# Choosing experts among 64 sums, four heads at a time, with Pool left out

## The chip, the cores and the metric

One Trainium2 chip, one core of it. The time is that of one execution of the whole program in microseconds on the device; three runs were taken, and the median stands for the kernel. Engines are named as in the profile: PE is TensorE, DVE is VectorE, ACT is ScalarE, POOL is GpSimd, SP issues most DMAs.

## What is computed

Two model blocks run one after the other on 512 tokens of width 1024. The change concerns the last part alone, a layer of experts (PEER). Each token has 8 heads. For each head two query halves are scored against 128 keys each; the best 16 of either side are taken, all 256 sums of one from each side are formed, and the best 16 sums name 16 experts and, by a softmax, their gates.

```python
s1, i1 = lax.top_k(sc[:, :, 0], 16)
s2, i2 = lax.top_k(sc[:, :, 1], 16)
cand = (s1[..., :, None] + s2[..., None, :]).reshape(ntok, 8, 256)
best, pos = lax.top_k(cand, 16)
e1 = take_along_axis(i1, pos // 16); e2 = take_along_axis(i2, pos % 16)
idx = e1 * 128 + e2                      # one of 16384 experts
gate = softmax(best)
act = gelu(u_tab[idx] . t) * gate        # per token: 128 experts
out = sum(act * v_tab[idx])
```

## The kernel before

The kernel is written in Tile: each instruction is put on an engine by hand, and the framework orders each engine's instructions by program order and by when their inputs are expected to be ready. An engine takes its queue in order, so an instruction that waits holds up what is behind it; instructions of a later part of the program may be placed ahead of earlier ones that are not ready yet.

The 512 tokens of the expert layer are four blocks of 128. Three of them (n = 0, 1, 2) take the dense way: for each of the 128 groups j of 128 experts, a first product of `u` with the 384 tokens and a GELU (`first_product`, L1724, 24 matmuls), the product with a gate matrix, and a second product with `v` that is summed up in PSUM (L1887). The fourth block (n = 3) gathers its experts' rows by indirect DMA and works on VectorE (L1846 to L1871).

Weights come in 128x1024 f32 tiles through `load_w` (L227 to L245): a DMA, a high half by ScalarE (L243), and a low half by a subtract (L244), which stands on VectorE unless `sub` names another engine. Of the three products that TensorE makes with each weight, one reads that low half.

The expert part has these stages.

1. Queries and scores (L1637 to L1767). `head_queries` makes the queries of a head from two weights, subtracted on Pool. For each head h and block n two matmuls give 128 tokens x 2 x 128 scores (L1750). For n = 0 in all heads, and for n = 1, 2 in heads 0 to 3, `choose` follows at once; the other scores are copied aside, those of n = 3 too. Nine first products (`FILLS`) are put between, subtracted on Pool.

2. `choose` (L1674) for one head: two searches for the best 16 of 128 (each two MAX8, two FIND_INDEX8 and a MATCH_REPLACE8), the 256 sums (L1691), a third search over these (L1693), the split of a position into its two flags (L1695 to L1699), a one-hot compare of both over 512 bf16 elements (L1701), a multiply with the keys on Pool (L1703) and a sum over the flags (L1704).

3. `spread` (L1770), for n = 0, 1, 2 in turn: softmax of the best sums (`soften`), three transposes, and then 32 steps. A step takes four tokens: VectorE makes two one-hot tiles of 128x512 (L1783, L1784), the gate is multiplied into the first (in even steps by four ScalarE scalings, L1787; in odd ones by Pool, L1789), four matmuls give the tokens' 128x128 gate matrices (L1804), and ScalarE copies them to a stage tile (L1806) that goes to memory every eighth step. The one-hots run two steps ahead of the matmuls; each of the two has five buffers. Between the steps stand 21 first products and, in the steps with k % 8 == 4, the `choose` of a waiting head of block n + 1.

4. Second products with gathers (L1837 to L1927). `prepare` loads the gates of four expert groups at a time, multiplies them into the activations (L1882, the gates at a step of four elements), splits the result and loads the `v` weight. Between them stand the remaining first products and the gathers of the fourth block, whose eight heads are chosen one by one from the scores kept aside.

Of the kernel before, what the change touches and what calls it, by code (L numbers as in the profile page):

```python
# [185 lines left out]
def _program(tc, I, out, dbg, upto, layers, pools):  # L186
# [1434 lines left out]
    ND = 3  # L1621
# [8 lines left out]
    gd = dr.tile([ND, 128, 32, 128, 4], F32, name="gd")  # L1630
# [30 lines left out]
    def sixteens(pool):  # L1661

        t = pool.tile([128, 16, 16], BF16, name="iob")
        nc.gpsimd.iota(t, pattern=[[1, 16], [0, 16]], base=0, channel_multiplier=0,
                       allow_small_or_imprecise_dtypes=True)
        return t

    def selection(pool, bufs):

        best = pool.tile([128, 8, 16], F32, name="best", tag="best", bufs=bufs)  # L1670
        keys = pool.tile([128, 2, 8, 16], F32, name="keys", tag="keys", bufs=bufs)
        return best, keys

    def choose(pool, sel, h, sc):  # L1674

        best, keys = sel
        s2 = pool.tile([128, 256], F32, name="s2", tag="s2", bufs=1)
        vv = pool.tile([128, 2, 16], F32, name="vv", tag="vv", bufs=2)
        ii = pool.tile([128, 3, 16], U32, name="ii", tag="ii", bufs=2)

        def top16(v, i, src, tmp):
            nc.vector.max(v[:, 0:8], src)
            nc.vector.max_index(i[:, 0:8], v[:, 0:8], src)
            nc.vector.match_replace(tmp, v[:, 0:8], src, -3.0e38)
            nc.vector.max(v[:, 8:16], tmp)
            nc.vector.max_index(i[:, 8:16], v[:, 8:16], tmp)

        for s in range(2):
            top16(vv[:, s], ii[:, s], sc[:, s], s2[:, 128 * s:128 * s + 128])
        cd = pool.tile([128, 256], F32, name="cd", tag="cd", bufs=1)  # L1690
        nc.vector.tensor_tensor(cd.rearrange("p (a b) -> p a b", a=16), vv[:, 0, :, None].to_broadcast([128, 16, 16]),  # L1691
                                vv[:, 1, None, :].to_broadcast([128, 16, 16]), op=OP.add)
        top16(best[:, h], ii[:, 2], cd, s2)  # L1693
        ab = pool.tile([128, 2, 16], U32, name="ab", tag="ab", bufs=2)
        nc.vector.tensor_scalar(ab[:, 0], ii[:, 2], 4, None, op0=OP.logical_shift_right)  # L1695
        nc.vector.tensor_scalar(ab[:, 1], ii[:, 2], 15, None, op0=OP.bitwise_and)
        fl = pool.tile([128, 2, 2, 16], BF16, name="fl", tag="fl", bufs=2)
        nc.vector.tensor_copy(fl[:, 0], ab)
        nc.vector.tensor_copy(fl[:, 1], ii[:, 0:2])  # L1699
        oh = pool.tile([128, 2, 16, 16], BF16, name="oh", tag="oh", bufs=2)  # L1700
        nc.vector.tensor_tensor(oh, iob[:, None].to_broadcast([128, 2, 16, 16]),  # L1701
                                fl[:, 0, :, None, :].to_broadcast([128, 2, 16, 16]), op=OP.is_equal)
        nc.gpsimd.tensor_tensor(oh, oh, fl[:, 1, :, :, None].to_broadcast([128, 2, 16, 16]), op=OP.mult)  # L1703
        nc.vector.tensor_reduce(keys[:, :, h], oh.rearrange("p s j k -> p s k j"), axis=AX.X, op=OP.add)  # L1704
# [28 lines left out]
    iob = sixteens(p1)  # L1733
# [35 lines left out]

    def spread(n):  # L1770
        best, keys = sels[n]
# [21 lines left out]
        for k in range(32 + LEAD):  # L1793
# [5 lines left out]
            if m % 8 == 0:  # L1799
                st = p1.tile([128, 32, 32, 4], F32, name="stg", tag="stage", bufs=2)  # L1800
# [5 lines left out]
            nc.scalar.activation(st[:, :, t0:t0 + 4], pg4.rearrange("p (t g e) -> p g t e", t=4, e=4), AF.Copy)  # L1806
            yield
            if m % 8 == 7:
                q = m // 8
                nc.sync.dma_start(gd[n, :, :, 32 * q:32 * q + 32], st)  # L1810
# [9 lines left out]
    steps, w = 0, None  # L1820
    for n in range(ND):
        for k, _ in enumerate(spread(n)):
            if steps in plan:
                first_product(plan[steps], w=w)
            steps += 1
            if steps + AH in plan and n == 2:
                w = load_w(I["uT"][plan[steps + AH]])
            elif steps + AH in plan:
                w = load_w(I["uT"][plan[steps + AH]], sub=SUB)
# [8 lines left out]
    iob = sixteens(p2)  # L1838
# [7 lines left out]
    def gather_head(h):  # L1846
        choose(p2, gsel, h, SC[:, 2 * h:2 * h + 2])
# [120 lines left out]
```

## Time and profile before

| | |
|---|---|
| median of 3 runs | 3669.14 us (3663.05 to 3673.33) |
| profiled execution | 3662.47 us, its span 3660.7 us |
| PE busy | 3516.7 us (96%) |
| DVE busy | 2413.3 us (66%) |
| ACT busy | 1494.5 us (41%) |
| POOL busy | 954.5 us (26%) |
| mean granted clock | 0.983 of 2.4 GHz |

Busy times are unions of an engine's instructions; on PE they say that something was in the array, not that it ran at its best. The rows of the waits say how long the first engine stood still for the second, in how many places. The stages lie in the span like this: queries and scores from 2280 us to about 2447, spread to 2699, three last first products to 2714, second products and gathers to the end.

### The profile page before, as it was taken

Reading aid. Unit: us, or ns where it says so; the run is one execution under the profiler, and the core shown is the slowest. Engines: PE = TensorE matmul, PEld = TensorE weight load, DVE = VectorE, ACT = ScalarE, POOL = GpSimd, SP = SyncE. Lnnn points to the kernel's source line nnn. Section 1 sums busy time; section 2 is a strip of 40 time slices with the busy share of each in tenths; the row PEclk is TensorE's granted clock in tenths of the full one; section 3 lists DMA queues with packets and bytes.
Section 4 is the critical chain, followed back from the end, with each engine's and each line's share of the span. In section 5 each row is a group of like instructions: output and inputs, shape, how many; then the busy total and the mean of one; then the engine's idle time right before and its main releaser. Section 6 shows DMA issues by size and latency. Waiting matters only on the chain. (4 is left out here: it accounts for less than half of the span.)

```text
span 3660.7 us, 54336 instructions
## 1 busy us (share of the span) xinstructions
PE 3516.7 (96%) x21341; PEld 3187.1 (87%) x21341; DVE 2413.3 (66%) x4258; ACT 1494.5 (41%) x2675; POOL 954.5 (26%) x722
## 2 busy tenths in 40 slices
PE   8999999999999999999989999987889999999998
PEld 8999999999898877888868877877788999999987
DVE  6565344334857545443477745788989988888865
ACT  4464233223346433332342633335653444443433
POOL 4221120000512202000133221455433433333321
PEclk9999999999999999999999999998999999999999
DMA  4102232222320233223331031324479888888855
GB/s 135 65 30 75 94 122 87 93 88 92 117 81 30 68 105 127 92 93 97 104 105 53 30 109 64 113 84 133 139 219 348 328 320 312 312 316 325 321 203 181
DMA packets 185888, 531.43 MB, mean 145 GB/s; under 512 B 16416, under 2 KB 70048, under 8 KB 168992
## 3 DMA queue, kind: packets, MB, share of 16 engines
q1 hardware_dynamic: 150272, 367.67, 30.6%
q0 software_dynamic: 18432, 134.23, 9.2%
q10 hardware_dynamic: 16928, 26.06, 2.2%
q8 instruction: 168, 2.75, 0.3%
q14 instruction: 88, 0.72, 0.1%
HBM read 492.64 MB, written 35.19 MB: 144 GB/s over the span
## 5 line engine op out<-in xcount | busy, mean ns | idle before, releaser
L243 ACT ACTIVATE whi<-wraw 128x1024 fp32r<-128x1024 f32 x594 | 627.8, 1058 | 1048.6 <-PE g L263 636.6
L244 DVE TENSOR_TENSOR wlo<-wraw,whi 128x1024 fp32r<-128x1024 f32 x543 | 680.1, 1253 | 296.3 <-ACT whi L243 282.3
L263 PE MATMUL g<-uh,whi 128*128 128x264 f32 (+1 forms) x1864 | 470.9, 315 | 4.4 <-ACT z L617 3.2
L263 PE MATMUL g<-uh,wlo 128*128 128x264 f32 (+1 forms) x1864 | 465.0, 312 | 1.3 <-DVE wlo L244 1.3
L263 PE MATMUL g<-ul,whi 128*128 128x264 f32 (+1 forms) x1864 | 465.3, 312 | 0.0
L350 POOL TENSOR_TENSOR ssq<-ssq,sq 128x512 f32<-128x512 f32 (+2 forms) x84 | 131.9, 1570 | 924.3 <-issue 716.7
L1730 PE MATMUL f<-TH,wlo 128*128 128x384 f32 x1024 | 349.9, 342 | 5.6 <-POOL wlo L244 5.6
L1730 PE MATMUL f<-TH,whi 128*128 128x384 f32 x1024 | 351.9, 344 | 1.1 <-ACT stash L1731 1.1
L1730 PE MATMUL f<-TL,whi 128*128 128x384 f32 x1024 | 348.5, 340 | 0.0
L263 PEld LDWEIGHTS g<-uh,whi 128*128 128x128 f32 x1864 | 305.2, 189 | 23.9 <-ACT z L617 3.6
L263 PEld LDWEIGHTS g<-uh,wlo 128*128 128x128 f32 x1864 | 305.0, 189 | 20.1 <-DVE wlo L244 1.5
L263 PEld LDWEIGHTS g<-ul,whi 128*128 128x128 f32 x1864 | 305.2, 189 | 17.9
L1913 POOL COPY pace<-al 1x1 f32<-1x1 f32 x128 | 110.5, 864 | 559.5 <-DVE al L332 557.7
L1892 PE MATMUL acc<-whi,ah 128*128 128x512 f32 x768 | 239.7, 394 | 4.6 <-ACT whi L243 3.9
L1892 PE MATMUL acc<-wlo,ah 128*128 128x512 f32 x768 | 239.0, 393 | 4.9 <-DVE wlo L244 4.9
L1892 PE MATMUL acc<-whi,al 128*128 128x512 f32 x768 | 238.0, 391 | 0.0
L263 PE MATMUL g<-Hh,wlo 128*128 128x264 f32 (+1 forms) x768 | 204.0, 320 | 0.0
L263 PE MATMUL g<-Hl,whi 128*128 128x264 f32 (+1 forms) x768 | 203.8, 320 | 0.0
L263 PE MATMUL g<-Hh,whi 128*128 128x264 f32 (+1 forms) x768 | 203.4, 319 | 0.0
L1730 PEld LDWEIGHTS f<-TH,wlo 128*128 128x128 f32 x1024 | 196.5, 192 | 6.6 <-POOL wlo L244 6.6
L1730 PEld LDWEIGHTS f<-TH,whi 128*128 128x128 f32 x1024 | 197.1, 193 | 5.8 <-ACT stash L1731 1.8
L1862 POOL DMA_INDIRECT gtile<-in_uv_dram,ix x128 | 190.0, 1484 | 46.4 <-issue 27.3
(593 smaller groups left out, 7579.4 us busy)
## 6 DMA issues: line engine op xcount, KB each, us to landing
wraw<-in_w_dram SPq DMA_DIRECT2D x340, 512.0 KB, 3.5
wraw<-in_uT_dram SPq DMA_DIRECT2D x128, 512.0 KB, 6.0
wraw<-in_uv_dram SPq DMA_DIRECT2D x128, 512.0 KB, 5.0
gd<-stg SPq DMA_DIRECT2D x12, 2048.0 KB, 9.7
gin<-gd SPq DMA_DIRECT2D x32, 768.0 KB, 8.5
h0c<-in_h_dram SPq DMA_DIRECT2D x8, 264.0 KB, 4.0
H<-in_h_dram ACTq DMA_DIRECT2D x8, 264.0 KB, 5.2
hs<-H ACTq DMA_DIRECT2D x8, 264.0 KB, 2.1
```

The lines of the kernel that those rows point to most:

```text
L243: nc.scalar.activation(hi, raw, AF.Copy)
L244: (sub or nc.vector).tensor_tensor(lo, raw, hi.bitcast(F32), op=OP.subtract)
L263: nc.tensor.matmul(pw, wt[:, sl], xt[:, kc, hf * w_:(hf + 1) * w_], start=(first and n == 0 and a == 0), stop=(last and n == len(kcs) - 1 ...
L350: nc.gpsimd.tensor_tensor(self.acc, self.acc, t, op=OP.add)
L1730: nc.tensor.matmul(p[:, :NT], wt[:, sl], x[:, kc], start=(kc == 0 and a == 0), stop=(kc == 7 and a == 2))
L1862: nc.gpsimd.indirect_dma_start(out=gtile, out_offset=None, in_=I["uv"], in_offset=bass.IndirectOffsetOnAxis(ap=ix[:, k:k + 1], axis=0))
L1892: nc.tensor.matmul(accs[2 * n + q], x[:, tk], wt[:, 512 * q:512 * q + 512], start=(j == 0 and k == 0), stop=(j == 127 and k == 2))
L1913: after = nc.gpsimd.tensor_copy(pace, ready[2][0:1, 0:1].bitcast(F32)).ins
```

## The change

- `choose` is split into `sides` (the two searches over 128, one head) and `pairs` (the rest, for nh heads). nh is 4 for the dense blocks and 1 for the gathered one. In stage 1 the pairs follow head 3 (and head 7 for n = 0); in `spread` the sides stand in the steps k = 2, 8, 14, 20 and the pairs in k = 26.
- `pairs` forms only 64 of the 256 sums: the first of one side with all 16 of the other, the next three with 8, the next four with 4, the last eight with 1. A position is turned into its two flags by thresholds and a bit mask. The key of the first side is found by a compare with the group bounds and a sum of differences of neighbouring keys, that of the second by a one-hot compare; both are multiplied on VectorE and summed by four halvings.
- All weight subtracts, the gate multiply and the key multiply of stages 1 to 3 go from Pool to VectorE. ScalarE now scales the gates in two of three steps, VectorE in the third. The one-hot tiles have four buffers each in place of five.
- The gate matrices lie in memory as [block, p, group, 4, (e, 32 tokens)]; the stage tile is written in that order, and the product in `prepare` reads runs of 32 tokens.

```diff
-            gemm2(p, load_w(sub=nc.gpsimd), uh, ul)
+            gemm2(p, load_w(), uh, ul)
-    gd = dr.tile([ND, 128, 32, 128, 4], F32, name="gd")
+    gd = dr.tile([ND, 128, 32, 4, 128], F32, name="gd")
+    def steps(pool):                       # replaces sixteens
+        t = pool.tile([128, 2, 16, 16], BF16, name="iob")
+        for a, z, width, o in PAIRS:
+            nc.gpsimd.iota(t[:, 0, a:z], pattern=[[width, z - a], [0, 16]], base=o, ...)
+        nc.gpsimd.iota(t[:, 1], pattern=[[1, 16], [0, 16]], base=0, ...)
+    PAIRS = ((0, 1, 16, 0), (1, 4, 8, 16), (4, 8, 4, 40), (8, 16, 1, 56))
+    def sides(pool, sel, h, sc, nh):
+        if h % nh == 0:
+            sel[2][0] = (pool.tile([128, nh, 2, 16], F32, name="vv", tag="vv", bufs=3),
+                         pool.tile([128, nh, 2, 16], U32, name="ii", tag="ii", bufs=3))
+        vv, ii = sel[2][0]
+        for s in range(2):
+            top16(pool, vv[:, h % nh, s], ii[:, h % nh, s], sc[:, s])
+    def pairs(pool, sel, h0, nh):
+        hs = slice(h0, h0 + nh)
+        best, keys, (vv, ii) = sel[0][:, hs], sel[1][:, :, hs], sel[2][0]
+        cd = pool.tile([128, nh, 64], F32, name="cd", tag="cd", bufs=1)
+        for a, z, width, o in PAIRS:
+            shape = [128, nh, z - a, width]
+            nc.vector.tensor_tensor(cd[:, :, o:o + (z - a) * width].rearrange("p h (a b) -> p h a b", b=width),
+                                    vv[:, :, 0, a:z, None].to_broadcast(shape),
+                                    vv[:, :, 1, None, :width].to_broadcast(shape), op=OP.add)
+        at = pool.tile([128, nh, 16], U32, name="at", tag="at", bufs=1)
+        for h in range(nh):
+            top16(pool, best[:, h], at[:, h], cd[:, h])
...
+        nc.vector.tensor_copy(fl[:, 0], at)
+        for k, (end, bits) in enumerate(((16, 8.0), (40, 4.0), (56, 3.0))):
+            nc.vector.tensor_scalar(mk[:, k], fl[:, 0], float(end), bits, op0=OP.is_lt, op1=OP.mult)
+        nc.vector.tensor_tensor(mk[:, 0], mk[:, 0], mk[:, 1], op=OP.add)
+        nc.vector.tensor_tensor(mk[:, 0], mk[:, 0], mk[:, 2], op=OP.add)
+        nc.vector.tensor_copy(mu[:, 0], mk[:, 0])
+        nc.vector.tensor_tensor(mu[:, 1], mu[:, 0], at, op=OP.bitwise_and)
+        nc.vector.tensor_copy(fl[:, 1], mu[:, 1])
+        nc.vector.tensor_copy(kb[:, 0:2], ii.rearrange("p h s k -> p s h k"))
+        nc.vector.tensor_copy(kb[:, 2, :, 0:1], kb[:, 0, :, 0:1])
+        nc.vector.tensor_tensor(kb[:, 2, :, 1:], kb[:, 0, :, 1:], kb[:, 0, :, :15], op=OP.subtract)
+        for s, op, src in ((0, OP.is_le, kb[:, 2]), (1, OP.is_equal, kb[:, 1])):
+            oh = pool.tile([128, nh, 16, 16], BF16, name="oh", tag="oh", bufs=1)
+            half = pool.tile([128, nh, 8, 16], BF16, name="half", tag="half", bufs=1)
+            nc.vector.tensor_tensor(oh, iob[:, s, None].to_broadcast(shape),
+                                    fl[:, s, :, None, :].to_broadcast(shape), op=op)
+            nc.vector.tensor_tensor(oh, oh, src[:, :, :, None].to_broadcast(shape), op=OP.mult)
+            nc.vector.tensor_tensor(half, oh[:, :, 0::2], oh[:, :, 1::2], op=OP.add)
+            nc.vector.tensor_tensor(oh[:, :, :4], half[:, :, 0::2], half[:, :, 1::2], op=OP.add)
+            nc.vector.tensor_tensor(half[:, :, :2], oh[:, :, 0:4:2], oh[:, :, 1:4:2], op=OP.add)
+            nc.vector.tensor_tensor(keys[:, s], half[:, :, 0], half[:, :, 1], op=OP.add)
-    OFF, AH, SUB, WH = 1, 1, nc.gpsimd, 4
+    OFF, AH, WH = 1, 1, 2
-    BYACT = lambda k: k % 2 == 0
+    BYACT = lambda k: k % 3 < 2
-                choose(p1, sels[n], h, sc)
+                sides(p1, sels[n], h, sc, 4)
+                if h % 4 == 3:
+                    pairs(p1, sels[n], h - 3, 4)
-            first_product(next(fill), nc.gpsimd)
+            first_product(next(fill))
-            oa = p1.tile([128, 4, 128], F32, name="oa", tag="oa", bufs=5)
+            oa = p1.tile([128, 4, 128], F32, name="oa", tag="oa", bufs=4)
-                nc.gpsimd.tensor_tensor(oa, oa, sl[:, 0, b:b + 4, None].to_broadcast([128, 4, 128]), op=OP.mult)
+                nc.vector.tensor_tensor(oa, oa, sl[:, 0, b:b + 4, None].to_broadcast([128, 4, 128]), op=OP.mult)
-            nc.scalar.activation(st[:, :, t0:t0 + 4], pg4.rearrange("p (t g e) -> p g t e", t=4, e=4), AF.Copy)
+            nc.scalar.activation(st[:, :, :, t0:t0 + 4], pg4.rearrange("p (t g e) -> p g e t", t=4, e=4), AF.Copy)
-            if n < ND - 1 and k % 8 == WH:
-                h = 4 + k // 8
-                choose(p1, sels[n + 1], h, wait[n + 1, h])
+            if n < ND - 1 and k % 6 == WH:
+                h = 4 + k // 6
+                if h < 8:
+                    sides(p1, sels[n + 1], h, wait[n + 1, h], 4)
+                else:
+                    pairs(p1, sels[n + 1], 4, 4)
-        choose(p2, gsel, h, SC[:, 2 * h:2 * h + 2])
+        sides(p2, gsel, h, SC[:, 2 * h:2 * h + 2], 1)
+        pairs(p2, gsel, h, 1)
-        nc.vector.tensor_mul(a, a, gins[0][:, :, :, j % 4].rearrange("p n t -> p (n t)"))
+        a4 = a.rearrange("p (n q t) -> p n q t", n=ND, q=4)
+        nc.vector.tensor_mul(a4, a4, gins[0][:, :, :, j % 4])
```

## Rows read from the trace of the kernel before

**Rows 1.** Busy time by stretch of us: length, engines with counts, granted clock, DMA share, GB/s
```profile
2315.20:2383.70 68.50, 68.19 (x331) 57.41 (x330) 61.01 (x263) 23.55 (x33) 33.40 (x19) 1.00 0.33 104
...
2640.80:2698.80 58.00, 48.99 (x348) 47.61 (x348) 57.26 (x66) 39.64 (x101) 26.51 (x18) 0.97 0.64 192
...
2714.00:2800.00 86.00, 78.66 (x377) 69.64 (x376) 75.02 (x125) 30.12 (x48) 22.57 (x19) 0.96 0.87 306
...
2900.00:3500.00 600.00, 600.00 (x3035) 546.32 (x3035) 535.93 (x892) 242.69 (x410) 233.28 (x176) 1.00 0.84 321
2383.70:2698.80 315.10, 258.89 (x1585) 247.02 (x1584) 291.11 (x696) 163.25 (x371) 162.88 (x92) 0.91 0.43 128
```

**Rows 2.** Waits of TensorE, 2296 to 2714 us: total, times, longest
```profile
PE s L1804 <- POOL oa L1789: 26.7, 19, 4.2
PE s L1804 <- DVE ob L1784: 10.9, 7, 3.5
...
PE f L1730 <- POOL wlo L244: 5.6, 3, 3.1
```

**Rows 3.** Waits of VectorE, 2383.7 to 2698.8 us
```profile
DVE keys L1704 <- POOL oh L1703: 11.6, 14, 1.9
DVE oa L1783 <- PE s L1804: 9.5, 4, 3.1
```

**Rows 4.** Groups of VectorE, same stretch: count | busy us, mean ns | idle, releasers
```profile
L1783 DVE TENSOR_TENSOR oa<-io,sl 128x512 f32<-128x512 f32 x96 | 98.0, 1021 | 9.8 <-PE s L1804 9.5 <-ACT sl L1777 0.3
L1784 DVE TENSOR_TENSOR ob<-io,sl 128x512 f32<-128x512 f32 x96 | 80.6, 840 | 0.0
L1704 DVE TENSOR_REDUCE keys<-oh 128x32 f32<-128x512 bf16 x16 | 17.9, 1117 | 11.6 <-POOL oh L1703 11.6
...
L244 DVE TENSOR_TENSOR wlo<-wraw,whi 128x1024 fp32r<-128x1024 f32 x5 | 6.0, 1217 | 0.8 <-ACT whi L243 0.8
```

**Rows 5.** Timeline of VectorE near 2345 us: start, duration, what
```profile
2343.20 0.29 DVE L1683 FIND_INDEX8 ii<-vv,s 128x8 uint32<-128x128 f32 x1
2343.40 0.07 DVE L1686 MATCH_VALUE_LOAD ii<-vv,s 128x8 f32 x1
2343.46 0.29 DVE L1686 FIND_INDEX8 ii<-vv,s 128x8 uint32<-128x128 f32 x1
...
2346.43 0.42 DVE L1683 FIND_INDEX8 ii<-best,cd 128x8 uint32<-128x256 f32 x1
2346.77 0.07 DVE L1684 MATCH_VALUE_LOAD s<-best,cd 128x8 f32 x1
...
2348.26 0.17 DVE L1695 TENSOR_SCALAR ab<-ii 128x16 uint32<-128x16 uint32 x1
2348.34 0.17 DVE L1696 TENSOR_SCALAR ab<-ii 128x16 uint32<-128x16 uint32 x1
```

**Rows 6.** Timeline of VectorE at the first one-hots, 2457 us
```profile
2457.65 0.68 DVE L1784 TENSOR_TENSOR ob<-io,sl 128x512 f32<-128x512 f32 x1
2458.25 0.68 DVE L1783 TENSOR_TENSOR oa<-io,sl 128x512 f32<-128x512 f32 x1
```

**Rows 7.** Timeline of TensorE near 2490 us, a first product, then one-hots
```profile
2490.02 0.33 PE L1730 MATMUL f<-TL,whi 128*128 128x384 f32 x1
...
2490.19 0.33 PE L1730 MATMUL f<-TH,wlo 128*128 128x384 f32 x1
...
2490.88 3.73 PE L1804 MATMUL s<-ob,oa 128*128 128x128 f32 x32
```

**Rows 8.** Tile oh: one-hot compare of a choice, min/median/max ns
```profile
L1701 DVE TENSOR_TENSOR oh<-iob,fl x32: 405/415/1255, 2322.4 to 3450.9; 128x512 bf16<-128x512 bf16 x32
```

**Rows 9.** Groups of VectorE, 2714 to 2800 us, columns as in rows 4
```profile
L1882 DVE TENSOR_TENSOR stash<-stash,gin 128x384 f32<-128x384 f32 x36 | 29.0, 849 | 9.8 <-DMA gin<-gd 9.7
...
L332 DVE TENSOR_TENSOR al<-stash,ah 128x384 fp32r<-128x384 f32 x10 | 5.5, 553 | 0.2 <-ACT ah L331 0.2
```

**Rows 10.** Groups of ScalarE, 2457 to 2698.8 us: the gate scaling
```profile
L1787 ACT ACTIVATE oa<-oa,sl 128x128 f32<-128x128 f32 x192 | 62.9, 391 | 79.0 <-DVE oa L1783 78.8
```

More of the change, by code (lines that the diff above doesn't have):

```diff
@@ L1659, in _program @@
                 nc.vector.scalar_tensor_tensor(TT[:, sl], p, rcol[:, n:n + 1], gr, op0=OP.mult, op1=OP.mult)
-    def sixteens(pool):
-        t = pool.tile([128, 16, 16], BF16, name="iob")
-        nc.gpsimd.iota(t, pattern=[[1, 16], [0, 16]], base=0, channel_multiplier=0,
+    def steps(pool):
+        t = pool.tile([128, 2, 16, 16], BF16, name="iob")
+        for a, z, width, o in PAIRS:
+            nc.gpsimd.iota(t[:, 0, a:z], pattern=[[width, z - a], [0, 16]], base=o, channel_multiplier=0,
+                           allow_small_or_imprecise_dtypes=True)
+        nc.gpsimd.iota(t[:, 1], pattern=[[1, 16], [0, 16]], base=0, channel_multiplier=0,
                        allow_small_or_imprecise_dtypes=True)
         return t
+    PAIRS = ((0, 1, 16, 0), (1, 4, 8, 16), (4, 8, 4, 40), (8, 16, 1, 56))
     def selection(pool, bufs):
@@ L1671, in selection @@
         keys = pool.tile([128, 2, 8, 16], F32, name="keys", tag="keys", bufs=bufs)
[L1672 to L1686, printed above, removed]
-        for s in range(2):
[L1689 to L1704, printed above, removed]
@@ new lines, in selection, with top16 @@
+        return best, keys, {}
+    def top16(pool, v, i, src):
+        tmp = pool.tile([128, 128], F32, name="s2", tag="s2", bufs=1)[:, :src.shape[1]]
+        nc.vector.max(v[:, 0:8], src)
+        nc.vector.max_index(i[:, 0:8], v[:, 0:8], src)
+        nc.vector.match_replace(tmp, v[:, 0:8], src, -3.0e38)
+        nc.vector.max(v[:, 8:16], tmp)
+        nc.vector.max_index(i[:, 8:16], v[:, 8:16], tmp)
+    def sides(pool, sel, h, sc, nh):
[3 more added lines that the diff above has]
+        vv, ii = sel[2][0]
+        for s in range(2):
+            top16(pool, vv[:, h % nh, s], ii[:, h % nh, s], sc[:, s])
@@ new lines, in pairs @@
+    def pairs(pool, sel, h0, nh):
[10 more added lines that the diff above has]
+            top16(pool, best[:, h], at[:, h], cd[:, h])
+        fl = pool.tile([128, 2, nh, 16], BF16, name="fl", tag="fl", bufs=1)
+        mk = pool.tile([128, 3, nh, 16], BF16, name="mk", tag="mk", bufs=1)
+        mu = pool.tile([128, 2, nh, 16], U32, name="mu", tag="mu", bufs=1)
+        nc.vector.tensor_copy(fl[:, 0], at)
[6 more added lines that the diff above has]
+        nc.vector.tensor_copy(fl[:, 1], mu[:, 1])
+        kb = pool.tile([128, 3, nh, 16], BF16, name="kb", tag="kb", bufs=1)
+        nc.vector.tensor_copy(kb[:, 0:2], ii.rearrange("p h s k -> p s h k"))
+        nc.vector.tensor_copy(kb[:, 2, :, 0:1], kb[:, 0, :, 0:1])
+        nc.vector.tensor_tensor(kb[:, 2, :, 1:], kb[:, 0, :, 1:], kb[:, 0, :, :15], op=OP.subtract)
+        shape = [128, nh, 16, 16]
+        for s, op, src in ((0, OP.is_le, kb[:, 2]), (1, OP.is_equal, kb[:, 1])):
[8 more added lines that the diff above has]
+            nc.vector.tensor_tensor(keys[:, s], half[:, :, 0], half[:, :, 1], op=OP.add)
@@ L1731, in first_product @@
         nc.scalar.activation(act_tile(j), p[:, :NT], AF.Gelu_apprx_tanh)
-    iob = sixteens(p1)
+    iob = steps(p1)
     FILLS = [1, 0, 0, 1, 1, 2, 2, 2]
     SHARE = [8, 8, 5]
-    OFF, AH, SUB, WH = 1, 1, nc.gpsimd, 4
+    OFF, AH, WH = 1, 1, 2
     TAILF = 3
     LEAD = 2
-    BYACT = lambda k: k % 2 == 0
+    BYACT = lambda k: k % 3 < 2
     sels = [selection(p1, ND) for n in range(ND)]
@@ L1766, in _program @@
         for _ in range(FILLS[h]):
-            first_product(next(fill), nc.gpsimd)
+            first_product(next(fill))
     def spread(n):
-        best, keys = sels[n]
+        best, keys = sels[n][:2]
         soften(n, best)
@@ L1779, in ones_hot @@
         def ones_hot(b, by_act):
-            oa = p1.tile([128, 4, 128], F32, name="oa", tag="oa", bufs=5)
-            ob = p1.tile([128, 4, 128], F32, name="ob", tag="ob", bufs=5)
+            oa = p1.tile([128, 4, 128], F32, name="oa", tag="oa", bufs=4)
+            ob = p1.tile([128, 4, 128], F32, name="ob", tag="ob", bufs=4)
             iot = io[:, None, :].to_broadcast([128, 4, 128])
@@ L1799, in spread @@
             if m % 8 == 0:
-                st = p1.tile([128, 32, 32, 4], F32, name="stg", tag="stage", bufs=2)
+                st = p1.tile([128, 32, 4, 32], F32, name="stg", tag="stage", bufs=2)
             oa, ob = hot.pop(0)
@@ L1819, in _program @@
             plan[32 * n + 32 * k // len(here) + OFF] = j
-    steps, w = 0, None
+    done, w = 0, None
     for n in range(ND):
         for k, _ in enumerate(spread(n)):
[L1823 to L1829, printed above, removed]
-            if n < ND - 1 and k % 8 == WH:
-                h = 4 + k // 8
-                choose(p1, sels[n + 1], h, wait[n + 1, h])
+            if done in plan:
+                first_product(plan[done], w=w)
+            done += 1
+            if done + AH in plan:
+                w = load_w(I["uT"][plan[done + AH]])
+            if n < ND - 1 and k % 6 == WH:
[4 more added lines that the diff above has]
+                    pairs(p1, sels[n + 1], 4, 4)
     for j in last:
-        first_product(j, sub=nc.gpsimd)
+        first_product(j)
     pools.release(p1)
     p2 = wk = pools.alloc(name="p2", bufs=1)
-    iob = sixteens(p2)
+    iob = steps(p2)
     pools.release(ps2, psum=True)
@@ L1877, in prepare @@
         if j % 4 == 0:
-            gins[0] = p2.tile([128, ND, 128, 4], F32, name="gin", tag="gin", bufs=2)
-            nc.sync.dma_start(gins[0], gd[:, :, j // 4].rearrange("n p t e -> p n t e"))
+            gins[0] = p2.tile([128, ND, 4, 4, 32], F32, name="gin", tag="gin", bufs=2)
+            nc.sync.dma_start(gins[0].rearrange("p n q e t -> p n (q e t)"),
+                              gd[:, :, j // 4].rearrange("n p q x -> p n (q x)"))
         w = load_w(I["uv"][128 * j:128 * j + 128, D:], pool=p2)
         a = act_tile(j)
-        nc.vector.tensor_mul(a, a, gins[0][:, :, :, j % 4].rearrange("p n t -> p (n t)"))
+        a4 = a.rearrange("p (n q t) -> p n q t", n=ND, q=4)
+        nc.vector.tensor_mul(a4, a4, gins[0][:, :, :, j % 4])
         ah = p2.tile([128, NT], F32R, name="ah", tag="ah", bufs=2)
```

2 lines of the change are left out of this document (1 added, 1 removed).

## The prediction

> **What bounds the kernel now.** I read the page first: TensorE is busy 96% of the span, so only stretches in which it idles can give time back. The busy times by stretch [rows 1] say where these are. From 2900 to 3500 us (second product and gathers) TensorE is busy 600 us of 600, and from 2315 to 2384 us it is busy 68.19 of 68.5: work saved on VectorE there buys nothing. From 2383.7 to 2698.8 us TensorE is busy only 258.89 of 315.1, at a mean clock of 0.91, while VectorE is busy 291.11. So in these 315 us, which run from the scores of head 3 to the last one-hot tile, VectorE sets the pace.
>
> The waits agree. TensorE waits longest for Pool's gate multiply (26.7 us), then for VectorE's second one-hot (10.9 us), then for Pool's weight subtract (5.6 us) [rows 2]. VectorE itself waits 11.6 us for Pool's expert multiply and 9.5 us for TensorE [rows 3].
>
> The groups of VectorE [rows 4] show a second cost of Pool. The two one-hot compares take 1021 and 840 ns in the mean; in a place where Pool is still idle the same ones take 0.68 us and start 0.60 us apart [rows 6]. The excess is 96 x (1.021 - 0.68) + 96 x (0.840 - 0.68) = 48 us of busy time that is lengthened by Pool's work, not needed.
>
> **The change, part by part.** The prices [rows 5]: on VectorE a search over 128 elements lasts 0.29 us and lets the next instruction start 0.20 us after it, one over 256 lasts 0.42 and takes 0.34, one over 16 elements takes 0.08, a match load 0.06. That is about 0.065 us plus 1.05 ns per element between starts, or 0.08 us more for an instruction that needs the result in front of it. For 64 elements I estimate 0.13 and 0.21 us.
>
> *Sides* (two searches over 128, unchanged): 10 x 0.20 + 6 x 0.06 = 2.4 us.
>
> *Pairs* for four heads. Four adds over 256 elements in all: 0.5 us back to back, 0.85 with every duration exposed. Four searches over 64 in place of 256: 4 x (5 x 0.13 + 3 x 0.06) = 3.4, or 5.1. Twelve small steps that turn the position into two flags, and the differences of the keys: 1.4 or 2.4. Two one-hot chains: 1024 bf16 elements compared, multiplied, then halved four times. A bf16 compare of 512 takes 415 ns [rows 8], half the cost per element of the f32 ones, so 1024 start 0.60 apart. No row shows a multiply whose operand repeats one value over the innermost 16; it costs between 0.60 (as the compare) and 1.14 (as f32, from the 1217 ns of 1024 elements [rows 4]). I take 1.14, since the bf16 row has both operands run along the innermost axis. The chain is then 0.60 + 1.14 + 0.33 + 0.20 + 0.13 + 0.13 = 2.5, twice 5.1, with durations 6.0. Sum: 10.4 us if other work fills each gap, 14.4 if none does, 9.4 with the cheap multiply. In the trace an instruction of one search (L1686) follows one of another (L1683) at once [rows 5], so some gaps are filled, and I take 12.5 us.
>
> On that multiply the Trainium skill has a rule (VectorE: DVE Perf Modes, section "Mode 2×_1P — pack two bf16 into one 32-bit read"): two results a cycle need 16-bit data at a step of 1 or -1. A repeated value has step 0, so by it the multiply runs at the full cost, as I took it; no run here shows it. If it did not hold, the sum below would be 6 x 2 x 0.54 = 6.5 us shorter.
>
> *One-hots*: 96 x 2 compares x 0.60 = 115 us, unchanged in number. Their gate multiply moves from Pool to VectorE for 10 of 32 steps: 30 x 0.60 = 18 us. ScalarE takes 22 of 32 in place of 16: 72 more scalings of 0.39 us [rows 10], 28 us; it was busy 163.25 of 315.1 us [rows 1], so that hides, except in the last token block (below).
>
> *Weight subtracts*: 1.15 us between starts (1217 ns long [rows 4]). Before, 5 of them stood on VectorE in the stretch and the others on Pool. After, all are VectorE's: I count 30 (21 first products, 8 fills, 1 of the last queries), 34.5 us. What is queued behind each is the next compare, and TensorE waits for both.
>
> *A step that moves.* Before, heads 0 to 2 ran their whole choice in the stretch up to 2383.7 us, where it is hidden. After, the pairs of heads 0 to 3 run for all three token blocks once head 3's scores exist, so 9 x 3.9 us of hidden work (a whole choice is 6.3 us by these prices, of it 2.4 sides, 1.9 the search over 256 and 1.05 the reduction of [rows 4]) comes back as part of 3 x 12.5 us behind 2383.7 us. That eats most of what the smaller search saves.
>
> *Sum over VectorE from 2383.7 us on*: 15 sides 36.0, 6 pairs 75.0, compares 115.2, multiplies 18.0, subtracts 34.5, three softmaxes 3.6 (as before): 282 us busy, against 291.1. No Pool instruction is left in the stretch, so its 11.6 us of waits and the lengthened compares are gone. Waits for TensorE (9.5 us) and ScalarE (0.8) stay. What is late next is TensorE itself: a first product is 24 matmuls 0.17 us apart, 4.15 us, and four steps of one-hots 3.73 us [rows 7], 7.9 us in four steps at the 2.4 GHz clock, against some 8.5 us of VectorE (282, less 77 for the 7 sides, 4 pairs and 9 subtracts ahead of the one-hots, over 24 groups of four). At 1.2 GHz TensorE needs 15.8, and the clock of 0.91 says that about a fifth of the stretch ran so; with four one-hot buffers in place of five VectorE then waits. I put 8 us for that, bounds 0 and 30. Total 282 + 10.3 + 8 = 300 us against 315.1: 15 us gained.
>
> *Gates in runs*. In the 86 us after 2714, VectorE is busy 75.02 and TensorE idles 7.3 us [rows 1]. The gate product takes 849 ns there, 36 times; a subtract of the same size with contiguous operands takes 553 [rows 9]. 36 x 0.3 = 11 us less work, but VectorE also waits 9.7 us there for the gates to land, and that stays: I take 2 us, bounds 0 and 7. Later the saving is hidden behind a full TensorE. The single-head pairs in the gather part have 21 instructions more each, 1.7 to 3.4 us at 0.08 to 0.16, and save 1.05 us of search and the 1.1 us reduction: nothing, hidden by 600 of 600. The new layout of the store to memory has runs of the same 512 bytes, and its read 2 KB: nothing.
>
> Forecast: 15 + 2 = 17 us gained. The profiled execution spanned 3660.7 us and took 3662.47; the median of the runs is 3669.14, 6.7 us above. I set the gain off against the median: 3652 us.
>
> **Rivals.**
>
> *Slower: the pairs block the weights.* Behind head 3, three pairs (37.5 us) stand on VectorE in front of the subtracts that the fills of heads 3 and 4 need. TensorE has the two last query products (estimate from [rows 7]: 24 x 0.17 x 512/384 = 5.4 us each), one head's scores (16 matmuls of the one-hots' shape, 3.73/16 x 8 x 2 = 3.7 us at most) and at most one prepared weight (4.15 us): some 18 us of work. Then it stands about 20 us, its clock falls, and the scores of heads 4 to 7, which are queued behind the fills, come late. VectorE then finds nothing to do while TensorE makes up 7 fills at 4.15 to 8.3 us. Price: 32 us of idle VectorE in place of 0, so 3652 + 32 = 3684 us. It decides as soon as VectorE's idle time in the stretch goes over 315 - 282 = 33 us (24 now). For it: subtract and pairs share one in-order queue. Against: other work is let into the gaps of a chain [rows 5].
>
> *No difference: chains and ScalarE.* If the pairs have every gap exposed, 6 x 1.9 = 11 us go; in the last block ScalarE's 39.64 of 58 us [rows 1] grow by 24 x 0.39 = 9.4 to 49, beside VectorE's 32 x 1.2 + 6 + 5.8 = 50, too close to run without waits. The gain shrinks to 6 us or less: 3663. The Trainium skill speaks for this one (VectorE: DVE Perf Modes, "The TRN2 errata"): each instruction pays a fixed latency, so many small ones cost more than few large ones. Here small ones that don't need each other start 0.08 us apart [rows 5].
>
> *Faster than forecast.* Pairs at 10.4 us and no added wait for TensorE: 12.6 + 8 us more, so 37 us gained, 3632 us. With the cheap multiply and 7 us at the gates it ends at 3620.
>
> *The change doesn't do what it says*: Pool would still have rows in the stretch; then the compares stay long and VectorE gains nothing. I see no such instruction in the diff and give it no chance of its own.
>
> **How the numbers follow.** Forecast 0.42 (own range 3640 to 3664), no difference 0.22, faster 0.16, slower 0.20. Range for 8 in 10: from 3624, which cuts half a rival's tail, to 3684, the slower case. Within 0.3% is 3658 to 3680, about what runs of this kernel can tell apart. Faster: 0.16, most of 0.42 (without 0.04 above 3658) and 0.04 of the third: 0.58. Slower: 0.18 of 0.20. Same: 0.24.
>
> **What would show it.** Right: no Pool row between the first scores and the last one-hot; compares at 0.67 to 0.70 us in the mean; the time from head 3's scores to the last one-hot near 300 us with VectorE busy near 282; the gate product near 0.55 us. Wrong: that time at 315 or more; TensorE waiting over 15 us in all for the weight subtract, above all within 40 us of head 3's scores; pairs that take over 14 us; or VectorE idle over 33 us in the stretch.

## The result, and the profile after

The changed kernel takes 3611.23 us (median of 4 runs, 3606.96 to 3612.28) against 3671.14 (4 runs, 3663.05 to 3673.33) for the kernel before, taken beside it: a ratio of 0.9839 [0.9821, 0.9856] (in brackets the 95% interval). That is 58 to 60 us gained where 17 were forecast; the time lies below the forecast range (3624 to 3684). Every ratio below is to runs of the kernel before taken beside that run; their medians lie between 3666.35 and 3671.14, so a difference of two medians of under 5 us says little. Its profiled execution took 3606.96 us with a span of 3605.2, 55.5 us shorter than before. First its busy times:

```profile
PE 3497.9 (97%) x21341; PEld 3169.9 (88%) x21341; DVE 2336.7 (65%) x4500; ACT 1515.0 (42%) x2747; POOL 735.4 (20%) x606
```

Then the stretches that answer to [rows 1], with the same columns: up to head 3's scores, after the last one-hots, the gather part, and the stretch from head 3's scores to the last one-hot.

```profile
2310.50:2378.20 67.70, 67.70 (x330) 57.39 (x329) 38.96 (x158) 23.56 (x34) 0.00 (x0) 1.00 0.36 120
2672.90:2760.00 87.10, 86.44 (x435) 77.97 (x434) 74.38 (x157) 34.25 (x55) 28.56 (x21) 1.00 0.92 335
2850.00:3450.00 600.00, 599.83 (x3034) 545.97 (x3033) 513.30 (x1014) 240.33 (x408) 223.66 (x168) 1.00 0.83 319
2378.20:2649.30 271.10, 248.60 (x1586) 235.83 (x1585) 266.15 (x867) 184.51 (x439) 0.00 (x0) 0.97 0.46 139
```

The last row is the one to read: 271.1 us where it was 315.1, VectorE busy for all but 5 of them, no Pool instruction. The account of the 55.5 us is then 44.0 in this stretch; 5.5 ahead of it (head 3's scores come at 2378.2 in place of 2383.7); and 6.0 behind it. Of the 5.5, 4.0 are already there at 2252 us, in code that the change does not touch: the first L272 matmul with `Oh` starts at 2256.3 before, at 2252.3 after, and anywhere from 2252.3 to 2261.1 in the fourteen traces of this document. Those 4.0 us are scatter between executions.

The waits of TensorE from 2378.2 to 2672 us, and of VectorE in the stretch (total, times, longest), answer to [rows 2, 3]:

```profile
PE s L1841 <- DVE oa L1826: 9.4, 13, 2.1
PE f L1765 <- DVE wlo L244: 4.9, 4, 2.7
PE s L1841 <- ACT oa L1824: 4.5, 11, 1.7
```

```profile
DVE vv L1683 <- PE s L1785: 3.8, 1, 3.8
DVE oa L1820 <- PE s L1841: 2.0, 1, 2.0
DVE oa L1820 <- ACT sl L1814: 1.6, 1, 1.6
DVE smg L1747 <- ACT best L1746: 0.6, 1, 0.6
```

TensorE's 26.7 us of waiting for Pool's gate multiply has become 9.4 for VectorE's. Of VectorE's own waits the first (3.8 us) is the wait for head 3's scores itself and ends where the stretch begins; inside it only 4 us are left, where 22 stood before.

The groups of VectorE in the stretch (count | busy us, mean ns | idle ahead) answer to [rows 4]:

```profile
L1820 DVE TENSOR_TENSOR oa<-io,sl 128x512 f32<-128x512 f32 x96 | 65.7, 684 | 3.7 <-PE s L1841 2.0 <-ACT sl L1814 1.6
L1821 DVE TENSOR_TENSOR ob<-io,sl 128x512 f32<-128x512 f32 x96 | 65.6, 684 | 0.0
L244 DVE TENSOR_TENSOR wlo<-wraw,whi 128x1024 fp32r<-128x1024 f32 x30 | 36.5, 1215 | 0.0
L1826 DVE TENSOR_TENSOR oa<-oa,sl 128x512 f32<-128x512 f32 x30 | 20.5, 684 | 0.0
L1734 DVE TENSOR_TENSOR oh<-oh,kb 128x1024 bf16<-128x1024 bf16 x12 | 14.6, 1213 | 0.0
L1732 DVE TENSOR_TENSOR oh<-iob,fl 128x1024 bf16<-128x1024 bf16 x12 | 8.2, 685 | 0.0
```

Compares at 684 ns, 30 subtracts and 30 multiplies are what the prediction counted. The timeline of VectorE while the pairs run (start, duration, instruction) shows how other work fills the gaps of a chain:

```profile
2398.17 0.22 DVE L1684 FIND_INDEX8 at<-best,cd 128x8 uint32<-128x64 f32 x1
2398.30 0.21 DVE L1686 MAX8 best<-s 128x8 f32<-128x64 f32 x1
2398.43 0.21 DVE L1683 MAX8 best<-cd 128x8 f32<-128x64 f32 x1
...
2400.83 0.22 DVE L1687 FIND_INDEX8 at<-best,s 128x8 uint32<-128x64 f32 x1
2400.97 1.21 DVE L244 TENSOR_TENSOR wlo<-wraw,whi 128x1024 fp32r<-128x1024 f32 x1
2402.09 0.08 DVE L1685 MATCH_VALUE_LOAD s<-best,cd 128x8 f32 x1
```

The last steps of one head's search and the first of the next stand side by side, 0.13 us apart though each lasts 0.21, and a weight subtract is let in between two steps of a search. I added up, over the whole stretch, the time from each start on VectorE to the next start, by kind of work (together 267.3 us; the row of the stretch has 266.15):

| us in the stretch | forecast | after |
|---|---|---|
| six pairs | 75.0 | 61.2 |
| 15 sides | 36.0 | 36.3 |
| 192 compares | 115.2 | 115.4 |
| 30 gate multiplies | 18.0 | 18.0 |
| 30 weight subtracts | 34.5 | 34.0 |
| softmax | 3.6 | 2.4 |
| VectorE idle | 18.3 | 5.0 |

### The profile page after: what moved, and what is told of

Same layout as the page of the kernel before. It is cut to its first block, busy times and chain, and to the rows that moved or that the text cites. A ratio compares the mean times of both kernels' runs of the same rounds, so it can differ in the third digit from the quotient of the medians.

```text
span 3605.2 us, 54355 instructions
## 1 busy us (share of the span) xinstructions
PE 3497.9 (97%) x21341; PEld 3169.9 (88%) x21341; DVE 2336.7 (65%) x4500; ACT 1515.0 (42%) x2747; POOL 735.4 (20%) x606
## 5 line engine op out<-in xcount | busy, mean ns | idle before, releaser
L244 DVE TENSOR_TENSOR wlo<-wraw,whi 128x1024 fp32r<-128x1024 f32 x587 | 733.8, 1251 | 331.6 <-ACT whi L243 324.3
L1901 POOL DMA_INDIRECT gtile<-in_uv_dram,ix x128 | 201.6, 1575 | 102.7 <-DVE AC L1910 65.3
```

Source lines behind the costliest of these rows:

```text
L244: (sub or nc.vector).tensor_tensor(lo, raw, hi.bitcast(F32), op=OP.subtract)
L1901: nc.gpsimd.indirect_dma_start(out=gtile, out_offset=None, in_=I["uv"], in_offset=bass.IndirectOffsetOnAxis(ap=ix[:, k:k + 1], axis=0))
```

## The experiments

**Pool emptied alone.** The kernel before, with its old search and gate layout; the subtracts, the gate multiply (ScalarE in two steps of three) and the key multiply leave Pool.

```diff
-    BYACT = lambda k: k % 2 == 0
+    BYACT = lambda k: k % 3 < 2
-            first_product(next(fill), nc.gpsimd)
+            first_product(next(fill))
...
-                nc.gpsimd.tensor_tensor(oa, oa, sl[...], op=OP.mult)
+                nc.vector.tensor_tensor(oa, oa, sl[...], op=OP.mult)
```

> The kernel before with Pool emptied in the expert part and nothing else changed: weight subtracts, gate multiply (ScalarE in two of three steps) and key multiply on VectorE, the search still over 256 sums, one head at a time. Theory A (VectorE paces the stretch from head 3's scores to the last one-hot, and Pool cost it lengthened compares and waits): VectorE needs 226 us by start-to-start prices for the old work, + 29 subtracts, + 18 gate multiplies, + 10 key multiplies = 283 us there, with 5 to 10 idle as in the changed kernel, so the stretch falls from 315 to 288 to 293 us and the time by 22 to 30 us, to about 3645. Compares at 0.68 us. Theory B (the gain is the smaller search): within 10 us of the kernel before, since VectorE only takes over work. Theory C (what the change gave is TensorE's clock): half-clock time in the stretch falls with the gain, and the gain is above 30 us.

Measured: 3636.98 us, ratio 0.9914 [0.9899, 0.993]. Its stretch, columns as above:

```profile
2388.20:2673.40 285.20, 255.43 (x1582) 241.29 (x1582) 283.11 (x778) 183.69 (x438) 0.00 (x0) 0.95 0.44 133
```

More work on VectorE, and yet 30 us less in the stretch: 283 us busy in place of 291, and 2 idle in place of 24. So some 31 of the 58 us need neither the smaller search nor the new layout. That is theory A's side, a little above its 22 to 30 us. Theory C (TensorE's clock) is not ruled out by this run, since the granted clock rose too, from 0.91 to 0.95; the run with the searches twice decides on it.

**The search with Pool at work.** The changed kernel, with subtracts and half the gate multiplies back on Pool.

```diff
-    BYACT = lambda k: k % 3 < 2
+    BYACT = lambda k: k % 2 == 0
-            first_product(next(fill))
+            first_product(next(fill), nc.gpsimd)
...
-                nc.vector.tensor_tensor(oa, oa, sl[...], op=OP.mult)
+                nc.gpsimd.tensor_tensor(oa, oa, sl[...], op=OP.mult)
```

> The changed kernel with Pool's weight subtracts and Pool's gate multiply (every other step) put back as before; the new search and key multiply stay on VectorE. Theory A: VectorE loses 25 subtracts (29 us) and 30 multiplies (18 us) of its 266 busy us, but the compares grow to about 0.85 to 1.0 us again (50 us in all) and TensorE waits for Pool's multiply 20 us or more, so the stretch is about 290 to 300 us: 19 to 29 us slower than the changed kernel, 3630 to 3640. Theory B: at most 10 us slower than the changed kernel (3621 or less).

Measured: 3664.01 us, ratio 0.9989 [0.9978, 1.0]. Its stretch, then groups of VectorE in it, then of Pool:

```profile
2383.30:2706.10 322.80, 259.39 (x1594) 247.37 (x1592) 304.87 (x812) 167.68 (x376) 150.82 (x75) 0.90 0.41 124
```

```profile
L1820 DVE TENSOR_TENSOR oa<-io,sl 128x512 f32<-128x512 f32 x96 | 90.8, 946 | 10.6 <-PE s L1841 8.8 <-ACT sl L1814 1.8
L1821 DVE TENSOR_TENSOR ob<-io,sl 128x512 f32<-128x512 f32 x96 | 82.5, 859 | 0.0
L1734 DVE TENSOR_TENSOR oh<-oh,kb 128x1024 bf16<-128x1024 bf16 x12 | 19.3, 1607 | 0.0
...
L1726 DVE COPY kb<-kb 128x4 bf16<-128x4 bf16 x6 | 6.2, 1034 | 0.0
```

```profile
L244 POOL TENSOR_TENSOR wlo<-wraw,whi 128x1024 fp32r<-128x1024 f32 x27 | 71.3, 2644 | 76.7 <-ACT whi L243 75.1 <-ACT oa L1824 1.5
```

The expectation, which left the rest of the change some 30 us of its own, was wrong: without Pool emptied the rest gains 4 us in the median, and the stretch is even 7.7 us longer than in the kernel before. With 25 subtracts and 30 multiplies fewer than in the changed kernel, VectorE is busy 38.7 us longer. A copy of four elements takes 1034 ns in the mean where it takes 160 in the changed kernel:

```profile
L1726 DVE COPY kb<-kb 128x4 bf16<-128x4 bf16 x6 | 1.0, 160 | 0.0
```

**Each half of Pool's work by itself.** The changed kernel with only the subtracts back on Pool (the `first_product` and `load_w` lines above), and with only the multiplies back (the `BYACT` and `tensor_tensor` lines).

> The changed kernel with only the weight subtracts of the expert part back on Pool (as in the kernel before); gate multiply stays on VectorE and ScalarE. Takes 25 x 1.15 = 29 us from VectorE's 266 busy us in the stretch from head 3's scores to the last one-hot, and puts about 70 us of Pool work beside it. Theory A1 (any Pool work with two inputs lengthens VectorE's, at the rate of the kernel before, 62 us per 163 us of Pool): 27 us come back as longer instructions, so the time stays within 10 us of the changed kernel's 3611, and TensorE waits more for the low weight half. Theory A2 (it was Pool's gate multiply alone, which stands between the one-hots and TensorE): 15 to 29 us faster, 3582 to 3596.

> The changed kernel with only the gate multiply of every other step back on Pool; all subtracts stay on VectorE. VectorE loses 30 x 0.6 = 18 us, ScalarE 28 us. Theory A1: 75 us of Pool work lengthen VectorE's by 28 us, and TensorE waits for Pool's multiply as before (25 to 33 us, partly hidden): 10 to 30 us slower than the changed kernel, 3621 to 3641. Theory A2: 25 to 45 us slower, 3636 to 3656, most of the change's gain gone. If VectorE's instruction count alone counted: 18 us faster.

Measured: 3636.59 us, 0.9903 [0.9886, 0.992], and 3636.51 us, 0.9902 [0.9886, 0.9919]. Each loses 25 us to the changed kernel, together nearly the 53 of the run above, so neither alone is the cause. For the subtracts both theories missed: A1 allowed 10 us, A2 expected a gain. For the multiplies the 25 us lie in A1's range. The stretch and the Pool group with the subtracts back:

```profile
2387.70:2677.40 289.70, 247.67 (x1586) 237.83 (x1585) 285.01 (x842) 179.58 (x434) 88.31 (x25) 0.94 0.43 129
```

```profile
L244 POOL TENSOR_TENSOR wlo<-wraw,whi 128x1024 fp32r<-128x1024 f32 x25 | 88.3, 3536 | 198.6 <-ACT whi L243 198.6
```

And with the multiplies back the stretch, the Pool group, and the longest wait of TensorE and of VectorE:

```profile
2386.00:2682.50 296.50, 252.42 (x1586) 239.60 (x1585) 280.55 (x838) 168.97 (x373) 86.13 (x48) 0.94 0.43 130
```

```profile
L1826 POOL TENSOR_TENSOR oa<-oa,sl 128x512 f32<-128x512 f32 x48 | 87.0, 1816 | 294.1 <-DVE oa L1820 267.0 <-ACT oa L1824 27.1
```

```profile
PE s L1841 <- POOL oa L1826: 24.4, 16, 4.9
```

```profile
DVE oa L1820 <- PE s L1841: 13.1, 8, 3.1
```

The two lose in different ways. With the subtracts on Pool VectorE does not wait (4.7 us idle), but it is busy 18.9 us longer with 25 subtracts fewer. With the multiplies on Pool it is busy 14.4 us longer and also idles 16, because TensorE waits for Pool and then VectorE for TensorE. The start-to-start sums say what grew (us):

| | after | subtracts back | multiplies back | both back |
|---|---|---|---|---|
| six pairs | 61.2 | 82.4 | 63.9 | 95.1 |
| 192 compares | 115.4 | 136.3 | 140.4 | 158.8 |

Pool's subtracts alone lengthen the pairs by 21 us and the compares by 21; they save VectorE 25 x 1.13 = 28. The sides, which are searches with one tensor in, stay as they are: 36.3 us, 36.3, 36.6 and 37.2 in the four columns. The Trainium skill says that GpSimd shares its SBUF interfaces with VectorE, and that VectorE's instructions with two SBUF inputs contend (GPSIMD Engine Reference, section "8. Key points"). These runs agree, and here the loss is larger than the work that Pool takes off.

**The gates in runs**, alone on the kernel before, and taken away from the changed kernel.

```diff
-    gd = dr.tile([ND, 128, 32, 128, 4], F32, name="gd")
+    gd = dr.tile([ND, 128, 32, 4, 128], F32, name="gd")
...
-        nc.vector.tensor_mul(a, a, gins[0][:, :, :, j % 4].rearrange("p n t -> p (n t)"))
+        a4 = a.rearrange("p (n q t) -> p n q t", n=ND, q=4)
+        nc.vector.tensor_mul(a4, a4, gins[0][:, :, :, j % 4])
```

> The kernel before with nothing but the gate matrices in runs of 32 tokens. Theory A: the gate product falls from 0.84 to 0.55 us, the only place where it counts is the first 90 us of the second products, where TensorE then idles 1 us in place of 4 and loses no clock: 5 to 7 us faster, 3664 to 3666. Rival: within 2 us, as VectorE waits for the gates to land anyway.

> The changed kernel with the old layout of the gate matrices. Theory A: 5 to 8 us slower than the changed kernel (3616 to 3619), all of it in the 90 us after the first second product. Rival: within 2 us of it (3611), and the 7 us that the changed kernel gains behind the last one-hot come from elsewhere.

Measured: alone 3663.38 us, 0.9982 [0.9973, 0.9992], so 5 us (12 runs against 23); undone 3618.3 us, 0.9871 [0.9855, 0.9886], 7 us over the changed kernel. Both as expected. The 5 us rest on the medians: in the trace of that run nothing is gained from the first second product to the end (939.9 us, 940.0 before), while undone takes 941.4 us there and the changed kernel 932.1. The 45 us that begin 45 us after the first second product, undone and in the changed kernel:

```profile
2718.10:2763.10 45.00, 40.85 (x193) 35.30 (x192) 44.80 (x60) 13.34 (x24) 14.06 (x10) 0.96 0.89 313
```

```profile
2718.10:2763.10 45.00, 44.34 (x223) 39.82 (x222) 40.83 (x66) 15.74 (x27) 16.49 (x12) 1.00 0.95 347
```

With the old layout VectorE is full there and TensorE idles 4.15 us; with the runs VectorE has room. VectorE's wait for the gates to land, in the 97 us that begin 7 us before the first second product, in the kernel before, with the runs alone, and undone:

```profile
DVE stash L1882 <- DMA gin<-gd: 9.9, 4, 5.9
DVE stash L1884 <- DMA gin<-gd: 12.1, 6, 5.9
DVE stash L1921 <- DMA gin<-gd: 0.2, 1, 0.2
```

Alone, what the shorter product saves is in part waited away; in the changed kernel with the old layout there was next to no such wait to begin with. The product itself, in the changed kernel (min/median/max ns), stands against the mean of 849 in [rows 9]:

```profile
L1923 DVE TENSOR_TENSOR stash<-stash,gin x128: 543/551/560, 2668.1 to 3460.4; 128x384 f32<-128x384 f32 x128
```

**The four searches twice.** The changed kernel; the second pass repeats the first.

```diff
-        for h in range(nh):
+        for h in [*range(nh)] * (2 if nh == 4 else 1):
```

> The changed kernel with the four searches over 64 sums made twice in each pair of the dense blocks (the same result twice): 6 x 4 x (5 x 0.13 + 3 x 0.06) = 20 us more VectorE work in the stretch, nothing else changed. Theory A (VectorE still paces it): 18 to 21 us slower, 3629 to 3632. Theory C (what holds the changed kernel is TensorE with its clock, VectorE only looks full): under 8 us slower.

Measured: 3625.39 us, 0.9882 [0.9865, 0.9898], 14 us over the changed kernel. Its stretch:

```profile
2380.10:2668.80 288.70, 250.99 (x1588) 236.84 (x1587) 286.80 (x1059) 183.58 (x440) 0.00 (x0) 0.96 0.44 133
```

Busy time grew by 20.65 us, 3.4 for the four searches of one pair (what the prediction took), and 17.6 of it lengthened the stretch: work on VectorE there costs nearly its full time. The 14 us are fewer than the 18 to 21 of theory A, but well over the 8 at most of theory C, by which TensorE with its clock would hold the changed kernel.

**Heads 0 to 3 paired two at a time.** The prediction said that pairing them only after head 3 moves hidden work into the stretch. Here heads 0 and 1 are paired after head 1's scores; the tiles keep their size for four heads.

```diff
-                sides(p1, sels[n], h, sc, 4)
-                if h % 4 == 3:
-                    pairs(p1, sels[n], h - 3, 4)
+                nh = 2 if h < 4 else 4
+                sides(p1, sels[n], h, sc, nh)
+                if h % nh == nh - 1:
+                    pairs(p1, sels[n], h + 1 - nh, nh)
...
```

> The changed kernel with heads 0 to 3 paired two at a time (after heads 1 and 3) in place of four: half of that work, three pairs of 5.2 us, moves into the stretch before head 3's scores, where TensorE is full and VectorE idles 29 of 68 us; each pair of two costs 0.8 us more than half a pair of four. Theory A: VectorE has 13 us less to do behind head 3's scores, so 10 to 13 us faster, 3598 to 3601. Theory C: within 5 us of 3611. It also tests the step of the prediction that work moved behind head 3's scores is paid in full.

Measured: 3598.74 us, 0.9805 [0.9788, 0.9821], 12.5 us better than the changed kernel, as expected. Up to head 3's scores, and the stretch:

```profile
2313.40:2381.80 68.40, 68.05 (x330) 57.36 (x329) 56.37 (x290) 23.75 (x33) 0.00 (x0) 1.00 0.35 112
2381.80:2639.90 258.10, 240.31 (x1586) 227.54 (x1585) 253.88 (x819) 184.06 (x439) 0.00 (x0) 1.00 0.48 147
```

VectorE does 17 us more ahead of head 3's scores, at no cost to a TensorE that is full there, and 12 less behind them.

**Heads 0 to 2 together, head 3 alone.** By the same reasoning this should hide more. The edit is shown against the twos.

```diff
-                nh = 2 if h < 4 else 4
+                nh, h0 = (3, 0) if h < 3 else (1, 3) if h == 3 else (4, 4)
...
```

> The changed kernel with heads 0 to 2 paired after head 2 and head 3 alone after head 3: behind head 3's scores stand three single pairs (3 x 3.3 us) in place of three pairs of two (3 x 6.0). Theory A: VectorE has 8 us less there than in twos, and room for it before (56 of 68 us busy in twos): 5 to 8 us faster than twos, 3591 to 3594. Rival: TensorE's floor or late sides, within 3 us of 3599.

Measured: 3608.57 us, 0.9842 [0.9822, 0.9862]: a miss, no better than fours (5 to 8 us better than twos were expected). Between head 1's, head 2's and head 3's scores:

```profile
2337.40:2361.00 23.60, 23.60 (x114) 19.82 (x114) 12.51 (x52) 7.78 (x11) 0.00 (x0) 1.00 0.33 110
2361.00:2385.40 24.40, 23.86 (x113) 19.73 (x112) 23.59 (x137) 6.64 (x9) 0.00 (x0) 1.00 0.20 63
```

VectorE idles half of the first gap and fills the second, and two of the three triple pairs still end after 2385.4 us (their last sums start at 2389.40 and 2400.68). A hidden place is only worth the idle time that VectorE has in it; twos use both gaps.

**More scaling on ScalarE**, with twos: five steps of six (the first of these runs) and all steps (the second).

```diff
-    BYACT = lambda k: k % 3 < 2
+    BYACT = lambda k: k % 6 < 5
```

> Heads 0 to 3 in twos (3598.7 us before) and ScalarE scaling the gates in five of six steps in place of two of three: 15 multiplies go from VectorE (9 us of its 254 busy us in the stretch), 60 scalings of 0.39 us come to ScalarE (184 to 207 of 258). Theory A (VectorE still paces, ScalarE has room): 6 to 9 us faster, 3590 to 3593. Rival (TensorE, 240 of 258 us busy, is the floor already): within 3 us of 3599.

> As the run before, with ScalarE scaling all gates: VectorE has 18 us less than in twos, ScalarE 47 us more (231 us of a stretch of 240 to 258). Theory A with ScalarE as the next bound: no better than five of six, within 5 us of it on either side, with TensorE waiting for the scaled one-hots. If ScalarE never binds: 3580 to 3584.

Measured: 3596.5 us, 0.9804 [0.9787, 0.9821], not to be told from twos, where 6 to 9 us were expected; and 3603.91 us, 0.9823 [0.9803, 0.9843], 7 us above five of six, where 5 at most were expected. With all steps, the part of the stretch from 2500 us on, and the longest waits of TensorE from 2382 us to the first second product (2665 us):

```profile
2500.00:2637.30 137.30, 127.56 (x862) 122.19 (x861) 121.06 (x282) 133.96 (x363) 0.00 (x0) 1.00 0.61 182
```

```profile
PE f L1770 <- ACT whi L243: 8.2, 6, 3.6
PE f L1770 <- DVE wlo L244: 7.9, 11, 2.2
```

ScalarE is busy 133.96 of 137.3 us, and the high halves of the weights come late. The loss is not in the stretch, which at 254.5 us is 3.6 us shorter than with twos, but behind it: the first second product starts 27.7 us after the last one-hot, with twos 24.4. Twos, with two of three or five of six steps on ScalarE, are the best of the versions run. For five of six it stays open why the median gains so little: in its profiled execution (3589.67 us; the other three take 3595.82 to 3597.3) the last one-hot ends 379.5 us after the first L272 matmul with `Oh`, with twos 384.7, so TensorE was not yet the floor that the rival took it for.

**Three one-hot buffers** in place of four, for both tiles, in the changed kernel.

```diff
-            oa = p1.tile([128, 4, 128], F32, name="oa", tag="oa", bufs=4)
+            oa = p1.tile([128, 4, 128], F32, name="oa", tag="oa", bufs=3)
...
```

> The changed kernel with three buffers for each one-hot tile in place of four. The prediction put 8 us (0 to 30) on VectorE waiting for TensorE with four in place of five; the trace of the changed kernel shows 2 us. If VectorE is ahead by buffers only rarely (theory A): within 4 us of 3611. If the depth carries it: over 10 us slower.

Measured: 3614.17 us, 0.9854 [0.9836, 0.9871], 3 us over the changed kernel, as expected. VectorE's wait for TensorE in the stretch grows from 2.0 to 4.6 us:

```profile
DVE oa L1820 <- PE s L1841: 4.6, 4, 2.2
```

So the buffers hold up next to nothing, and the 8 us that the prediction set aside for them were not there.

## Why the prediction was right in its mechanism and wrong in its size

Its mechanism was right: VectorE sets the pace from head 3's scores to the last one-hot, Pool's work lengthens VectorE's, and the sum over VectorE gives the stretch. Three sizes were off, all to the same side, and with them the sum.

1. *Pairs at 12.5 us.* They took 61.2/6 = 10.2, the lower end of what was worked out (10.4 if other work fills each gap). The step that failed is "some gaps are filled": nearly all are; four heads' searches, sides and weight subtracts are there to be let in, as the timeline shows. That is 13.8 us of the 29 by which the stretch was missed (300 against 271). The multiply was taken at its right price: 1213 ns for 1024 bf16 elements with a repeated operand, against 685 for the compare of the same size. There the Trainium skill's rule on steps of 1 or -1 (VectorE: DVE Perf Modes, section "Mode 2×_1P — pack two bf16 into one 32-bit read") and the trace agree.

2. *Idle at 10.3 + 8 us.* It was 5.0, which is 13 us more. The 10.3 carried the old waits for TensorE over as if they were TensorE's own; the run with only the multiplies back brings them back (13.1 us) together with TensorE's wait for Pool (24.4), and with Pool emptied alone VectorE does not wait for TensorE at all, so they were Pool's, at second hand. The 8 for half clock and four buffers was not there: VectorE waits 2.0 us for TensorE with four and 4.6 with three. TensorE's granted clock in the stretch rose to 0.97 from 0.91.

3. *Gates in runs at 2 us.* They gave 7 on top of the rest, the upper bound. The step that failed is that the wait for the gates "stays". It does on the kernel before (9.9 us, 12.1 with the runs alone). In the changed kernel with the old layout it is 0.2 us and VectorE is full (44.80 of 45 us), so what the product saves is TensorE's at once. Why the gates land in time there is open.

The 5.5 us ahead of head 3's scores were not forecast, and 4.0 of them are scatter, as said above. One wait was passed over: TensorE's 9.2 us for the softmax (L1714) stands between the 10.9 and the 5.6 in the order of the waits; no term of the sum hangs on it.

Right were the counts (30 subtracts, 30 multiplies, 192 compares), the compares at 0.68 us, ScalarE's room in two steps of three, the gather part (600 of 600 before, 599.83 after), and the step that moves: taking a part of it back gained 12.5 us.

Of the rivals, *slower* fell: TensorE waits 4.9 us in all for a weight subtract, and VectorE idles 5 us, not 33. *No difference* fell: the chains are not exposed, and ScalarE is full only when it scales in all steps. *Faster than forecast* came nearest and named the pairs, the added wait for TensorE and the gates, but kept the 10.3 us of old waits and stopped at 3632, or 3620 with a cheap multiply that did not come. *Doesn't do what it says* fell by the column of Pool.

Taken as steps, the 58 us are some 31 for the emptied Pool, 19 for the smaller search four heads at a time on top of that (3636.98 to 3618.3), and 7 for the gates. The traces bear this out to within some 4 us (us; from the first L272 matmul with `Oh` to the end of the last one-hot, and from the first second product to the end):

| | to the last one-hot | second products |
|---|---|---|
| before | 442.5 | 940.0 |
| Pool emptied alone | 415.2 | 939.2 |
| gates undone | 396.1 | 941.4 |
| changed kernel | 397.0 | 932.1 |
| gates alone | 443.3 | 939.9 |
| Pool back | 449.5 | 933.3 |

The order matters: with Pool at work, search and gates together gain 4 (3664.01 against 3668.26), and the traces show a gain in the second products alone.

## What to carry to other kernels

Where one engine sets the pace and a second takes work off it, first ask what the second engine's work adds to the first's instructions; where that is near the cost of the work taken off or above it (here 47 us against 28 for the subtracts), do it all on the first. When pricing a batch of short chains on an engine that is never short of other work, take the time from start to start, not a middle between filled and exposed. And put batched work where the pacing engine idles ahead of the critical stretch: the batch size that fills that idle time (twos here) beats both the larger ones.

## What was not expected of the hardware

- 88 us of Pool's subtracts (25 of 3.54 us mean) beside a VectorE that is hardly ever idle lengthened VectorE's other work by some 47 us (18.9 us more busy, with 25 x 1.13 us of subtracts gone): about half a microsecond for each microsecond of Pool's. Pool's own subtract went from 2.47 us in the kernel before to 3.54 in this run.
- A very small instruction can suffer most: the copy of 128x4 took 160 ns in the changed kernel, 503 with the subtracts on Pool, 1034 with the multiplies there too, and 156 with the multiplies alone.
- In the run with Pool emptied alone, VectorE's compares took 703 ns and its subtracts 1236, 2 to 3% more than in the changed kernel (684, 1215), with no Pool work beside them. It cost nothing: from start to start the 192 compares took 115.3 us there and 115.4 in the changed kernel.
